# The first FFN's down projection computed as 2x2 blocks with seven block products

## The chip, the cores and the metric

The kernel runs on one core of a Trainium2 chip. The metric is the device time of one execution in microseconds (us), as a median of repeated executions; beside it stands one execution that the hardware profiler recorded. Engines are named as the profile names them: PE (TensorE, matmuls), PEld (its weight loads), DVE (VectorE), ACT (ScalarE), POOL (GpSimd), SP (SyncE, which here only issues DMAs).

## The reference

One residual block on 512 tokens of width 1024: a feed-forward part (FFN1), a token mixer, and a second feed-forward part (FFN2), each between RMS norms. The change touches the first of these lines:

```python
def swiglu(x, w_gu, w_down):
    g, u = jnp.split(x @ w_gu, 2, axis=-1)
    return (jax.nn.silu(g) * u) @ w_down

f = swiglu(rms_norm(h, ffn1_pre_g[l]), ffn1_w_gu[l], ffn1_w_down[l])
h = h + MACARON_SCALE * rms_norm(f, ffn1_post_g[l])
m = hybrid_mixer(rms_norm(h, mix_pre_g[l]), ...)
```

The hidden width (ff) is 2816, which is 22 chunks of 128. `w_down` is 2816 by 1024.

## The kernel before

**Numbers.** Every fp32 operand is split into a high part (rounded to the fp32r type, an ACT copy) and a low part (what is left, a DVE subtract). One product is three matmuls: high by high, high by low, low by high (`mm3`, lines 134 to 137). Each new operand therefore costs one cast on ACT and one subtract on DVE before PE can use all of it. Weights come in the order of a list (`worder`), through a small set of buffers: SP loads `wraw`, ACT and DVE make `w` (`wsplit`, lines 101 to 109).

**FFN1, gate and up.** The first 6 pairs of ff chunks ("standard", tiles f1f and f1g) are ordinary products; the other 16 pairs go in `paired` (tiles f1X, f1Y, f1Q) as 2x2 blocks with seven products instead of eight. The tiles f1W are its split weights, f1M and f1N sums of weight blocks, and u1m and u1ts the sums and splits of the normalised input that this form needs. The hidden activations end in tiles f1p, four chunks in each.

**FFN1, down.** `token_out` (lines 585 to 617) walks over the 22 ff chunks. For each chunk it takes one weight w (128 by 1024) and the split chunk of activations (ph, pl), and for four token blocks and two halves of the output it runs `mm3` with 512 columns into eight accumulators f1o. The last 6 chunks (`TAILS[0]`) are held back: they are run token block by token block, so that the first block is complete early and its norm (`boundary`, name b1) runs beside the matmuls of the others. The b1 work of a token block is `post_norm` (a square with a sum on ACT, a scale on DVE for each half, then a small chain over DVE and POOL), `normalise`, and transposes on PE back to feature order (`to_features`, tiles b1ntp into u2h and u2l), from which the mixer's first products x start.

**FFN2, down.** It is already done in the other form, by the class `Blocked` (lines 469 to 579). Sixteen ff chunks form two groups; in each group the product of the (tokens by ff) block and the (ff by outputs) block is cut in 2x2 blocks, and seven block products replace eight. A product is four steps (two groups, two halves), 28 steps in all. Each step needs a split weight block f2w, and each product a split sum of activations f2a (`prep`); then `multiply` runs 12 matmuls with 512 columns into banks X, Y, Z and V. Between products, `add_up` adds weight blocks and activation blocks on DVE, POOL adds a weight block from memory with an accumulating DMA (line 538), and `snap` copies a bank aside when a product has to count in two outputs. At the end `post_norm` adds or subtracts that copy first (tile b3qz, line 213). The 6 ordinary chunks left over go into the same banks, the first two for all tokens, the last four token by token (`TAILS[2]` is 4). The steps of `Blocked` are issued in the order of the program text (`manual_schedule`); elsewhere a scheduler sets the order of each engine's queue.

**Short loads for the mixer.** `vec`, `sink`, `cs` and `msk` are loaded by SP after the fifth ordinary down weight (line 751); `hb` (DVE, line 758) and `z` (ACT, line 763) are the first users of `vec`.

Of the kernel before, what the change touches and what calls it, by code (L numbers as in the profile page):

```python
# [16 lines left out]
P = 128  # L17
LRU_LAG = (2, 2)
ATT_LAG = (3, 2)
TAILS = (6, 7, 4)  # L20
JSTD = {"f1": 6, "f2": 4}
GC = 4
NS = 4 * GC
LEAD = 3
PRODUCTS = (1, 2, 5, 6, 3, 7, 4)
BLOCKED = ("f2",)
FEATURE_LAG = {"b1": (3, 3, 3, 3), "b2": (3, 3, 3, 4)}
ATT_GATES = (2, 3, 4, 5, 6, 7)
T = 512
# [11 lines left out]


@with_exitstack
def hybrid_block_kernel(ctx, tc, x, xt, g1, w_first, gains, gu1, gs1, dn1, w_x, w_gate, w_q, w_k, w_v, w_gl, w_ga, w_pl, w_pa,
                        w_o, gu2, gs2, dn2, ds2, vecs, bd, sinks, rope, mask, out):
    nc = tc.nc
    V, A, G, PE, SP = nc.vector, nc.scalar, nc.gpsimd, nc.tensor, nc.sync
# [204 lines left out]
    def gate_up(u, name, first, fast, rs=None, ds=None):  # L252
        ps = {}
        sp = []
        base = NS if ds is not None else 0

        def pw(j):
            if j < base:
                key, slot, n = (j // (2 * GC), j % 2), j // 2 % GC, GC
            else:  # L260
                key, slot, n = (j - base) // 4, (j - base) % 4, 4
            if key not in ps:
                ps[key] = b8(f"{name}p{j}", [P, n, T])
            return ps[key][:, slot, :]

        def split(c):
            i = c - base
            if i % 4 == 0:
                sp.append((b8(f"{name}ph{i // 4}", [P, 4, T], F32R), b8(f"{name}pl{i // 4}", [P, 4, T], F32R)))
            split_chunk(ps[i // 4], *sp[-1], i % 4)  # L270

        def chunk(c):
            if c + 2 < KF and c >= base + 2:
                split(c + 2)
            return sp[(c - base) // 4]

        def tail(j, bg, bu):
            s = t2(f"{name}s{j}")
            if rs is not None:
                gs, us = t2(f"{name}gs{j}"), t2(f"{name}us{j}")  # L280
                V.tensor_tensor(out=gs, in0=bg, in1=rs(), op=ALU.mult)
                V.tensor_tensor(out=us, in0=bu, in1=rs(), op=ALU.mult)
                bg, bu = gs, us
            A.activation(s, bg, AF.Tanh, scale=0.5)
            V.scalar_tensor_tensor(out=s, in0=s, scalar=1.0, in1=bg, op0=ALU.add, op1=ALU.mult)
            V.scalar_tensor_tensor(out=pw(j), in0=s, scalar=0.5, in1=bu, op0=ALU.mult, op1=ALU.mult)

        bs = []

        def done(i, b):  # L290
            bs.append(b)
            if i % 2 == 1:
                tail(i // 2, bs[i - 1], b)

        first(u, f"{name}f", done)
        for j in range(2, JSTD[name]):
            bb = []
            for i in range(2):
                w = wget()
                b = bank(f"{name}g{j}{i}")  # L300
                feat_chunk(b, w, u, ALL)
                tick()
                bb.append(b)
            tail(j, *bb)
        while live:
            tick()
        blocked = None if ds is None else Blocked(name, ps, ds)
        ahead = iter(range(base, base + 4))
        paired(fast(), name, pw, blocked, lambda: split(next(ahead)))
        if blocked is None:  # L310
            for c in range(4):
                split(c)
        return chunk, blocked
# [305 lines left out]
    def boundary(src, dst, g_post, g_pre, u, scale, name, raw=None, then=None):  # L619
        rhs = []  # L620

        def residual():
            t = len(rhs)
            if t < NT:
                rh = b8(f"{name}rh{t}", [P, 2, D])
                A.dma_start(rh[:, 0, :], src[t])
                rhs.append(rh)

        residual()
        residual()  # L630

        def epilogue(t, banks, fix):
            residual()
            h = post_norm(banks, fix, t, g_post, rhs[t], scale, f"{name}q", dst[t] if g_pre is None else None)
            if g_pre is None:
                return
            un = normalise(h, t4(f"{name}un{t}"), t, g_pre, f"{name}n")
            A.dma_start(dst[t], h)
            yield FEATURE_LAG[name][t]
            to_features(un, t, u, f"{name}n", raw)  # L640
            if then is not None and t == NT - 1:
                start(then())

        return epilogue
# [93 lines left out]
        wsplit(2)  # L738
        start(token_scale(lambda: [done(i, b) for i, b in enumerate(bs)]))

    chunk1, _ = gate_up(u1, "f1", first_unscaled, lambda: (gs1, mv1), lambda: rbc)
    g_post, g_pre = gain_pair(1, 2, "g_b1")
    u2 = new_u("u2")
    hs = [dram.tile([P, D], F32, name=f"h_spill{t}") for t in range(NT)]
    token_out(chunk1, KF, boundary(xv, hs, g_post, g_pre, u2, 0.5, "b1"), "f1", TAILS[0])

    vec = const.tile([P, 8, KD], F32, name="vec")
    sink = const.tile([P, NH], F32, name="sink")
# [322 lines left out]
def _layout(inputs):  # L1071
    import numpy as np

    c = np.ascontiguousarray
    f = {k: np.asarray(v)[0] for k, v in inputs.items()}
    a = {}
    a["x"] = c(f["x"])
    a["xt"] = c(f["x"].T.reshape(KD, P, T))
    a["g1"] = c(f["ffn1_pre_g"].reshape(KD, P).T)
    a["w_first"] = None  # L1080
    a["gains"] = np.stack([f[n] for n in ("ffn1_pre_g", "ffn1_post_g", "mix_pre_g", "mix_post_g",
                                          "ffn2_pre_g", "ffn2_post_g")])

    def gu(w):
        return c(w.reshape(KD, P, 2, KF, P).transpose(3, 2, 1, 0, 4).reshape(KF, 2, P, D))

    def chunks(w):
        return c(w.reshape(KD, P, KD, P).transpose(2, 1, 0, 3).reshape(KD, P, D))

    a["w_first"] = c(f["ffn1_w_gu"].reshape(KD, P, 2, KF, P)[:, :, :, :2].transpose(0, 1, 3, 2, 4).reshape(KD, P, 512))  # L1090
    def pairs_of(w, j):
        b = w.reshape(2, 4, P, 2, KF // 2, 2, P).transpose(4, 3, 5, 0, 2, 1, 6)[j // 2:].reshape(-1, 2, 2, P, 512)
        return c(np.stack([np.concatenate([b[:, 0, 1], b[:, 0, 0]], 2), np.concatenate([b[:, 1, 0], b[:, 1, 1]], 2)], 1))

    a["gu1"], a["gs1"] = gu(f["ffn1_w_gu"])[2:JSTD["f1"]], pairs_of(f["ffn1_w_gu"], JSTD["f1"])
    a["dn1"] = c(f["ffn1_w_down"].reshape(KF, P, D))
    w = f["w_in"]
    a["w_x"], a["w_gate"] = chunks(w[:, D:2 * D]), chunks(w[:, :D])
    half = HD // 2

    def pairs(w):
        return w.reshape(D, -1, 4, 2, half).transpose(0, 1, 3, 2, 4).reshape(D, -1)

    def chunks_of(w):
        n = w.shape[1] // P
        return c(w.reshape(KD, P, n, P).transpose(2, 1, 0, 3).reshape(n, P, D))

    a["w_q"], a["w_k"] = chunks_of(pairs(w[:, 2048:3072])), chunks_of(pairs(w[:, 3072:3328]))
    a["w_v"] = c(w[:, 3328:3584].reshape(2, 4, P, 256).transpose(0, 2, 1, 3).reshape(2, P, 1024))
    a["w_gl"], a["w_ga"] = chunks(w[:, 3584:4608]), chunks(w[:, 4608:])  # L1110
    a["w_pl"] = chunks(f["w_proj_lru"])
    wa = f["w_proj_attn"].reshape(2, 2, 4, HD, D).transpose(0, 2, 1, 3, 4).reshape(D, D)
    a["w_pa"] = chunks(wa)
    a["w_o"] = c(f["w_out"].reshape(KD, P, D))
    a["gu2"], a["gs2"] = gu(f["ffn2_w_gu"])[:JSTD["f2"]], pairs_of(f["ffn2_w_gu"], JSTD["f2"])
    a["dn2"] = c(f["ffn2_w_down"].reshape(KF, P, D)[NS:])

    def quarters(w):
        b = w[:NS * P].reshape(2, 2, 2, 2, P, 2, 512)
        return c(b.transpose(0, 5, 3, 1, 4, 2, 6).reshape(2, 2, 2, 2, P, 1024))  # L1120

    q = quarters(f["ffn2_w_down"])
    a["ds2"] = c(np.stack([q[:, 0, 0], q[:, 1, 0], q[:, 0, 1], q[:, 1, 1]], 1))
    vec = [f["conv_w"][i] for i in range(4)] + [f[n] for n in _VECS]
    a["vecs"] = c(np.stack(vec).reshape(8, KD, P).transpose(2, 0, 1))
    bd = np.zeros((2, 2, HD, KD, 2, HD), np.float32)
    wb = np.stack([f["lru_w_a"], f["lru_w_x"]]).reshape(2, KD, 2, HD, HD)
    for r in range(2):
        bd[:, r, :, :, r, :] = wb[:, :, r].transpose(0, 2, 1, 3)
    a["bd"] = bd.reshape(2, P, D)  # L1130
    a["sinks"] = f["attn_sinks"]
    inv = (10000.0 ** (-np.arange(half) / half)).astype(np.float32)
    ang = np.arange(T, dtype=np.float32)[:, None] * inv[None, :]
    cs = np.stack([np.cos(ang), np.sin(ang)]).astype(np.float32).transpose(2, 0, 1)
    a["rope"] = c(np.tile(cs, (4, 1, 1)))
    qi, si = np.arange(P)[:, None], np.arange(2 * P)[None, :]
    a["mask"] = np.where((si > qi) & (si <= qi + P), 0.0, -1e30).astype(np.float32)
    return a
# [24 lines left out]
```

## Time and profile before

| | |
|---|---|
| median of 3 runs | 1149.4 us (1148.77 to 1150.24) |
| the profiled execution | 1149.67 us, of which its span is 1147.9 us |
| mean granted PE clock | 0.995 |
| ACT busy | 558.2 us (49% of the span) |
| POOL busy | 64.4 us (6%) |
| FFN1 start (first products, scaling) | to about 86 us |
| FFN1 gate and up, paired | 86 to 243.2 us |
| FFN1 down | 243.2 to 369.5 us |
| FFN2 gate and up, paired | 850 to 1026.4 us |
| FFN2 down, blocked | 1026.4 to 1097.5 us, then its tail to 1140 us |

The profile is of one execution. A row of a timeline has the start, the duration, the engine, the line, the operation, and output<-inputs with their shapes; in brackets stands the idle time before it and what ended that. [...] A row of the windows has, for each engine, the busy time in that stretch and the number of instructions, then the granted clock, the share of the DMA engines and GB/s.

### The profile page before, as it was taken

What the parts mean: (1) busy time and instruction counts of PE and PEld (TensorE: products, weight loads), DVE (VectorE), ACT (ScalarE), POOL (GpSimd) and SP (SyncE); (2) the same over time, 40 slices, a digit from 0 to 9 for tenths busy, and PEclk for the clock granted to TensorE, in tenths of its full rate; (3) what the DMA queues carried; (4) which work ended last, traced back from release to release, by engine and by line L of the source; (5) the groups of instructions that cost most, each with busy time, mean ns of one, the idle gap of its engine ahead of it and who ended that gap; (6) DMA issues with size and microseconds to landing.
All of it is one profiled execution on the core that took longest, in us unless ns stands there. A gap on an engine that the chain in (4) does not pass through costs nothing.

```text
span 1147.9 us, 16623 instructions
## 1 busy us (share of the span) xinstructions
PE 1121.6 (98%) x6632; PEld 999.0 (87%) x6632; DVE 847.0 (74%) x1216; ACT 558.2 (49%) x942; POOL 64.4 (6%) x66
## 2 busy tenths in 40 slices
PE   7979999999999999999999999999999999999997
PEld 6769999998888988888888888887989999998886
DVE  6598889975315787999867662455758989979866
ACT  7234545553313676566655441344435555455652
POOL 1000000000001010212211100000000000001000
PEclk9999999999999999999999999999999999999999
DMA  9123333274312545432632432432313333255632
GB/s 362 46 69 111 111 107 98 84 285 167 93 37 99 180 142 148 151 90 73 194 118 74 147 114 88 165 128 100 122 37 111 111 108 97 90 184 159 171 128 74
DMA packets 41757, 142.81 MB, mean 124 GB/s; under 512 B 5072, under 2 KB 5200, under 8 KB 41040
## 3 DMA queue, kind: packets, MB, share of 16 engines
q1 hardware_dynamic: 35920, 122.35, 33.2%
q10 hardware_dynamic: 4608, 15.21, 3.6%
q0 software_dynamic: 1152, 4.19, 1.9%
q8 instruction: 52, 0.85, 0.3%
q14 instruction: 25, 0.20, 0.1%
HBM read 130.20 MB, written 11.53 MB: 123 GB/s over the span
## 4 chain that ended last, share of the span: by engine, by line
PE 85%; DVE 10%; ACT 2%; issue 2%; DMA 1%; POOL 0%; DVEq 0%; POOLq 0%; ACTq 0%
PE f2X L136 4%; PE f2X L137 4%; PE f2X L135 4%; PE f1o L135 3%; PE f1o L137 3%; PE f1o L136 3%; PE f1X L135 3%; PE f1X L137 3%; PE f1X L136 3%; PE f1f L736 2%; PE f2Q L137 2%; PE f2Q L136 2%; PE f2Q L135 2%; DVE w L106 1%; PE f1Q L135 1%
## 5 line engine op out<-in xcount | busy, mean ns | idle before, releaser
L106 DVE TENSOR_TENSOR w<-wraw,w 128x1024 fp32r<-128x1024 f32 x112 | 136.4, 1248 | 44.8 <-ACT w L105 43.4
L105 ACT CAST w<-wraw 128x1024 fp32r<-128x1024 f32 x112 | 112.9, 1049 | 64.8 <-PE f1o L137 17.7
L135 PE MATMUL f1X<-u1m,f1W 128*128 128x256 f32 x256 | 73.1, 286 | 3.7 <-ACT f1sn L365 3.7
L137 PE MATMUL f1X<-u1m,f1W 128*128 128x256 f32 x256 | 73.2, 286 | 2.3 <-DVE f1W L345 2.3
L136 PE MATMUL f1X<-u1m,f1W 128*128 128x256 f32 x256 | 73.0, 285 | 0.0
L135 PE MATMUL f1o<-w,f1ph 128*128 128x512 f32 x176 | 68.5, 390 | 0.0
L136 PE MATMUL f1o<-w,f1ph 128*128 128x512 f32 x176 | 68.5, 389 | 0.0
L137 PE MATMUL f1o<-w,f1pl 128*128 128x512 f32 x176 | 67.0, 389 | 0.0
L135 PEld LDWEIGHTS f1X<-u1m,f1W 128*128 128x128 f32 x256 | 49.7, 194 | 4.0 <-ACT f1sn L365 3.9
L137 PEld LDWEIGHTS f1X<-u1m,f1W 128*128 128x128 f32 x256 | 49.6, 194 | 2.6 <-DVE f1W L345 2.5
L136 PEld LDWEIGHTS f1X<-u1m,f1W 128*128 128x128 f32 x256 | 49.7, 194 | 0.1
L137 PE MATMUL f2X<-u3m,f2W 128*128 128x256 f32 x144 | 40.8, 283 | 0.0
L137 PE MATMUL f2Q<-u3m,f2W 128*128 128x256 f32 x144 | 40.8, 283 | 0.0
L135 PE MATMUL f2Q<-u3m,f2W 128*128 128x256 f32 x144 | 40.8, 283 | 0.0
L136 PE MATMUL f2X<-u3l,f2W 128*128 128x256 f32 x144 | 40.8, 283 | 0.0
L137 PE MATMUL f2X<-u3h,f2W 128*128 128x256 f32 x144 | 40.8, 283 | 0.0
L136 PE MATMUL f2X<-u3m,f2W 128*128 128x256 f32 x144 | 40.8, 283 | 0.0
L136 PE MATMUL f2Q<-u3m,f2W 128*128 128x256 f32 x144 | 40.8, 283 | 0.0
L135 PE MATMUL f2X<-u3m,f2W 128*128 128x256 f32 x144 | 40.7, 283 | 0.0
L135 PE MATMUL f2X<-u3h,f2W 128*128 128x256 f32 x144 | 40.7, 283 | 0.0
L135 PEld LDWEIGHTS f1o<-w,f1ph 128*128 128x128 f32 x176 | 33.0, 188 | 6.9 <-ACT f1ph L249 0.2
L136 PEld LDWEIGHTS f1o<-w,f1ph 128*128 128x128 f32 x176 | 33.0, 188 | 6.9
(784 smaller groups left out, 3703.7 us busy)
## 6 DMA issues: line engine op xcount, KB each, us to landing
wraw<-in_dn_dram SPq DMA_DIRECT2D x28, 512.0 KB, 5.3
f2L<-in_gs_dram SPq DMA_DIRECT2D x18, 512.0 KB, 3.6
f2R<-in_gs_dram SPq DMA_DIRECT2D x18, 512.0 KB, 4.4
wraw<-in_gu_dram SPq DMA_DIRECT2D x16, 512.0 KB, 6.4
f1L<-in_gs_dram SPq DMA_DIRECT2D x16, 512.0 KB, 3.6
f1R<-in_gs_dram SPq DMA_DIRECT2D x16, 512.0 KB, 4.3
f2b<-in_ds_dram SPq DMA_DIRECT2D x16, 512.0 KB, 4.5
wraw<-in_w_x_dram SPq DMA_DIRECT2D x8, 512.0 KB, 4.5
```

The source lines that it names most:

```text
L105: A.copy(w[:, 0, :], raws[n])
L106: V.tensor_tensor(out=w[:, 1, :], in0=raws[n], in1=w[:, 0, :].bitcast(F32), op=ALU.subtract)
L135: PE.matmul(o, lhsT=ah, rhs=bh, start=start, stop=False, skip_group_check=reopen)
L136: PE.matmul(o, lhsT=ah, rhs=bl, start=False, stop=False, skip_group_check=reopen)
L137: PE.matmul(o, lhsT=al, rhs=bh, start=False, stop=stop, skip_group_check=reopen)
L736: PE.matmul(bs[i], lhsT=lw[:, i * P:(i + 1) * P], rhs=rx, start=k == 0 and n == 0, stop=k == KD - 1 and n == 2)
```

## The change

The class `Blocked` is given to FFN1 as well. `gate_up` gets the rearranged weights `ds1`; the host rearranges both down weights with one helper, `down`, and `dn1` now holds only 6 chunks.

```diff
-    chunk1, _ = gate_up(u1, "f1", first_unscaled, lambda: (gs1, mv1), lambda: rbc)
+    chunk1, blocked1 = gate_up(u1, "f1", first_unscaled, lambda: (gs1, mv1), lambda: rbc, ds1)
...
-    token_out(chunk1, KF, boundary(xv, hs, g_post, g_pre, u2, 0.5, "b1"), "f1", TAILS[0])
+    token_out(chunk1, KF, boundary(xv, hs, g_post, g_pre, u2, 0.5, "b1"), "f1", TAILS[0], blocked1)
...
-    a["dn1"] = c(f["ffn1_w_down"].reshape(KF, P, D))
+    a["dn1"], a["ds1"] = down(f["ffn1_w_down"])
...
-    a["dn2"] = c(f["ffn2_w_down"].reshape(KF, P, D)[NS:])
+    a["dn2"], a["ds2"] = down(f["ffn2_w_down"])
```

Since `TAILS[0]` stays 6 and six ordinary chunks are left, all six now run token by token. The 528 ordinary matmuls f1o become 480: 336 in the 28 steps (tiles f1X, f1Y, f1Z, f1V) and 144 in the tail. On DVE come 28 splits f1w, 14 splits f1a, 8 sums of activations, 8 sums of weights and 8 corrections b1qz; 16 splits of w and 16 of f1pl go. On ACT come 28 casts f1w, 14 casts f1a and 8 copies of a bank, and 16 casts of w and 16 of f1ph go. POOL gets 8 accumulating DMAs of 512 KB; SP gets 16 loads f1b and loses 16 loads wraw. One line lower than before stands everything below line 26 of the kernel, since an unused constant is gone.

Giving `ds1` also changes how `pw` places the activations: the tile f1p that a chunk is written to is now chosen by even and odd chunk, as `Blocked` reads them, and that shifts the scheduler's order in the first stage, whose code is the same. These are rows of DVE's queue in that first stage, before (w4 and w5 are the split weights of the standard chunk 4; f1gs, f1us, f1s, f1p steps of a chunk's activation; u1ts, u1m parts of the input for the paired products):

```order
L286 SCALAR_TENSOR_TENSOR f1p0_395<-f1s0_388,f1us0_390 128x512
L106 TENSOR_TENSOR w4_417<-wraw4_272,w4_417 128x1024
L659 TENSOR_TENSOR u1ts1_525<-xs1_78,u1ts0_524 128x1024
L281 TENSOR_TENSOR f1gs3_486<-f1g30_422,rbc_124 128x512
L106 TENSOR_TENSOR w5_451<-wraw5_321,w5_451 128x1024
L286 SCALAR_TENSOR_TENSOR f1p0_395<-f1s1_397,f1us1_399 128x512
```

And the same place of DVE's queue after the change:

```order
L285 SCALAR_TENSOR_TENSOR f1p0_395<-f1s0_388,f1us0_390 128x512
L658 TENSOR_TENSOR u1ts1_526<-xs1_78,u1ts0_525 128x1024
L280 TENSOR_TENSOR f1gs3_487<-f1g30_423,rbc_124 128x512
L284 SCALAR_TENSOR_TENSOR f1s2_410<-f1s2_410,f1gs2_411 128x512
L285 SCALAR_TENSOR_TENSOR f1p1_404<-f1s1_397,f1us1_399 128x512
L281 TENSOR_TENSOR f1us3_488<-f1g31_455,rbc_124 128x512
L105 TENSOR_TENSOR w4_418<-wraw4_272,w4_418 128x1024
L105 TENSOR_TENSOR w5_452<-wraw5_321,w5_452 128x1024
```

The split of w4 has moved behind one operation of 1024 columns and four of 512. Some thirty rows further on, at the entry of the paired stage, DVE's queue before reads (f1W20 is the weight of the third product of pair 0):

```order
L286 SCALAR_TENSOR_TENSOR f1p4_573<-f1s5_629,f1us5_631 128x512
L334 TENSOR_TENSOR f1M0_649<-f1R0_638,f1L0_637 128x512
L334 TENSOR_TENSOR f1M1_663<-f1R1_642,f1L1_641 128x512
L334 TENSOR_TENSOR f1N0_650<-f1R0_638,f1M0_649 128x512
L334 TENSOR_TENSOR f1N1_664<-f1R1_642,f1M1_663 128x512
L345 TENSOR_TENSOR f1W20_658<-f1M0_649,f1W20_658 128x1024
L345 TENSOR_TENSOR f1W11_669<-f1R1_642,f1W11_669 128x1024
```

After the change the same place reads:

```order
L333 TENSOR_TENSOR f1M0_649<-f1R0_638,f1L0_637 128x512
L281 TENSOR_TENSOR f1us5_631<-f1g51_604,rbc_124 128x512
L333 TENSOR_TENSOR f1M1_663<-f1R1_642,f1L1_641 128x512
L333 TENSOR_TENSOR f1N0_650<-f1R0_638,f1M0_649 128x512
L284 SCALAR_TENSOR_TENSOR f1s5_629<-f1s5_629,f1gs5_630 128x512
L344 TENSOR_TENSOR f1W20_658<-f1M0_649,f1W20_658 128x1024
L333 TENSOR_TENSOR f1N1_664<-f1R1_642,f1M1_663 128x512
L344 TENSOR_TENSOR f1W11_669<-f1R1_642,f1W11_669 128x1024
L370 TENSOR_TENSOR f1ca0_701<-f1Y0_673,f1sn0_699 128x256
L285 SCALAR_TENSOR_TENSOR f1p1_404<-f1s5_629,f1us5_631 128x512
```

Two operations of 512 columns, the sum f1N1 and the last f1p of chunk 5, now stand behind the split of f1W20, which so comes earlier by these two. The third place is the end of the blocked steps on DVE, where the six ordinary weights w8 to w13 are split (f1w411 is the last blocked weight; hb reads vec):

```order
L534 TENSOR_TENSOR f1w411_3140<-f1b111_2482,f1w411_3140 128x1024
L249 TENSOR_TENSOR f1pl0_3117<-f1p16_2235,f1ph0_3116 128x512
L757 TENSOR_SCALAR hb_3531<-vec_3523 128x16
L105 TENSOR_TENSOR w8_3157<-wraw8_3062,w8_3157 128x1024
L249 TENSOR_TENSOR f1pl0_3117<-f1p16_2235,f1ph0_3116 128x512 x2
L105 TENSOR_TENSOR w9_3194<-wraw9_3064,w9_3194 128x1024
L105 TENSOR_TENSOR w10_3215<-wraw10_3066,w10_3215 128x1024
L105 TENSOR_TENSOR w11_3220<-wraw11_3160,w11_3220 128x1024
L105 TENSOR_TENSOR w12_3225<-wraw12_3197,w12_3225 128x1024
L249 TENSOR_TENSOR f1pl1_3231<-f1p20_2710,f1ph1_3230 128x512 x2
L105 TENSOR_TENSOR w13_3234<-wraw13_3218,w13_3234 128x1024
```

Before, the split of an ordinary weight stood well ahead of its use all along the stage, and hb stood between two of them near its start:

```order
L373 TENSOR_TENSOR f1cb15_2522<-f1Q15_2482,f1sw15_2620 128x256
L758 TENSOR_SCALAR hb_3489<-vec_3481 128x16
L106 TENSOR_TENSOR w10_2677<-wraw10_2586,w10_2677 128x1024
L106 TENSOR_TENSOR w11_2714<-wraw11_2591,w11_2714 128x1024
L106 TENSOR_TENSOR w12_2743<-wraw12_2596,w12_2743 128x1024
```

Now hb, and with it the wait for vec's load, stands directly ahead of w8, and the other five splits follow it in one run.

More of the change, by code (lines that the diff above doesn't have):

```diff
@@ L25 @@
 PRODUCTS = (1, 2, 5, 6, 3, 7, 4)
-BLOCKED = ("f2",)
 FEATURE_LAG = {"b1": (3, 3, 3, 3), "b2": (3, 3, 3, 4)}
@@ L43, in hybrid_block_kernel @@
 @with_exitstack
-def hybrid_block_kernel(ctx, tc, x, xt, g1, w_first, gains, gu1, gs1, dn1, w_x, w_gate, w_q, w_k, w_v, w_gl, w_ga, w_pl, w_pa,
+def hybrid_block_kernel(ctx, tc, x, xt, g1, w_first, gains, gu1, gs1, dn1, ds1, w_x, w_gate, w_q, w_k, w_v, w_gl, w_ga, w_pl, w_pa,
                         w_o, gu2, gs2, dn2, ds2, vecs, bd, sinks, rope, mask, out):
@@ L1095, in _layout, with down @@
     a["gu1"], a["gs1"] = gu(f["ffn1_w_gu"])[2:JSTD["f1"]], pairs_of(f["ffn1_w_gu"], JSTD["f1"])
-    a["dn1"] = c(f["ffn1_w_down"].reshape(KF, P, D))
+    def down(w):
+        b = w[:NS * P].reshape(2, GC // 2, 2, 2, P, 2, 512).transpose(0, 5, 3, 1, 4, 2, 6).reshape(2, 2, 2, 2, P, 1024)
+        return c(w.reshape(KF, P, D)[NS:]), c(np.stack([b[:, 0, 0], b[:, 1, 0], b[:, 0, 1], b[:, 1, 1]], 1))
+    a["dn1"], a["ds1"] = down(f["ffn1_w_down"])
     w = f["w_in"]
@@ L1115, in _layout @@
     a["gu2"], a["gs2"] = gu(f["ffn2_w_gu"])[:JSTD["f2"]], pairs_of(f["ffn2_w_gu"], JSTD["f2"])
-    a["dn2"] = c(f["ffn2_w_down"].reshape(KF, P, D)[NS:])
[L1118 to L1123, printed above, removed]
+    a["dn2"], a["ds2"] = down(f["ffn2_w_down"])
     vec = [f["conv_w"][i] for i in range(4)] + [f[n] for n in _VECS]
```

## The prediction

> **What bounds the kernel now.** I read the page first: the busy shares, then the chain that ended last.
>
> ```profile
> PE 1121.6 (98%) x6632; PEld 999.0 (87%) x6632; DVE 847.0 (74%) x1216; ACT 558.2 (49%) x942; POOL 64.4 (6%) x66
> PE 85%; DVE 10%; ACT 2%; issue 2%; DMA 1%; POOL 0%; DVEq 0%; POOLq 0%; ACTq 0%
> ```
>
> PE is the bound over the whole, but 10% of the chain is DVE, so the average hides a stage with another limit. The windows, stage by stage, show which (start of FFN1, its down projection, FFN2's blocked down projection, and the token tail behind that):
>
> ```profile
> 43.00:86.00 43.00, 35.16 (x164) 28.91 (x163) 43.00 (x57) 17.34 (x22) 0.00 (x0) 1.00 0.17 49
> 243.20:369.50 126.30, 125.92 (x580) 104.97 (x580) 61.68 (x94) 45.41 (x74) 3.83 (x7) 1.00 0.37 131
> 1026.40:1097.50 71.10, 70.71 (x329) 58.71 (x328) 63.72 (x63) 42.70 (x50) 7.11 (x8) 1.00 0.55 146
> 1097.50:1140.00 42.50, 42.50 (x189) 35.18 (x189) 26.38 (x37) 12.98 (x25) 1.66 (x3) 1.00 0.30 111
> ```
>
> In the stage that is changed PE idles 0.38 of 126.3 us and DVE is half used (61.68): fewer matmuls shorten it one for one. FFN2, which already has the new form, is PE-bound too, but DVE works 63.72 of 71.1 us there. Between 43 and 86 us DVE is busy without a gap and PE waits. Last, the list of PE's waits:
>
> ```profile
> PE f1X L135 <- ACT f1sn L365: 3.7, 1, 3.7
> PE f1X L137 <- DVE f1W L345: 2.3, 1, 2.3
> PE f1g L137 <- DVE w L106: 1.9, 1, 1.9
> PE x L135 <- ACT u2h L199: 0.6, 2, 0.4
> PE f2X L136 <- DVE f2w L535: 0.4, 1, 0.4
> ```
>
> The first three lie in the start of FFN1; the blocked form has cost FFN2's PE one wait of 0.4 us.
>
> **The matmuls that go.** 528 become 480: 48 of 128x512 less. Their price is a distance between starts, not a duration. The page's group has the duration; the window is a stretch of the down projection in which PE does little else:
>
> ```profile
> L135 PE MATMUL f1o<-w,f1ph 128*128 128x512 f32 x176 | 68.5, 390 | 0.0
> 260.00:340.00 80.00, 80.00 (x355) 66.26 (x354) 29.80 (x39) 24.61 (x32) 0.00 (x0) 1.00 0.30 98
> ```
>
> 80 us over 355 matmuls is 0.2254 us each, against a duration of 0.390. So 48 x 0.2254 = 10.8 us. [...]
>
> **The 28 steps.** They add to DVE and ACT, and that work has to hide under 336 matmuls, 336 x 0.2254 = 75.7 us. FFN2 runs the same list of steps, with the same waits in its queues, so its rows price them: the split of a step, its share of the accumulating DMAs.
>
> ```profile
> L535 DVE TENSOR_TENSOR f2w<-f2b,f2w x28: 1212/1219/1226, 1019.4 to 1099.0; 128x1024 fp32r<-128x1024 f32 x28
> ACT f2w L534 <- DMA f2b<-in_ds_dram: 6.7, 3, 2.6
> ```
>
> DVE gets 28 + 14 + 8 + 8 operations of 1.22 us, 70.8 us, and beside them its share of the last paired products; it is nearly full, as in FFN2. ACT waited 6.7 us there for accumulated weights, and of all this 0.4 us reached PE, since steps are prepared three ahead. I take 0.4 us again; bounds 0 and, with one such DMA wait (2.6 us) reaching PE, 3 us.
>
> **The token tail.** Six weights must be there for the first token block, where FFN2 had two spread over all tokens and four. FFN2's end of the steps shows what DVE does behind the last blocked split and when PE is through with the steps:
>
> ```profile
> 1097.90 2.35 DVE L535 TENSOR_TENSOR f2w<-f2b,f2w 128x1024 fp32r<-128x1024 f32 x2
> 1100.77 1.21 DVE L106 TENSOR_TENSOR w<-wraw,w 128x1024 fp32r<-128x1024 f32 x1
> 1103.11 4.62 DVE L106 TENSOR_TENSOR w<-wraw,w 128x1024 fp32r<-128x1024 f32 x4
> 1107.65 1.28 DVE L250 TENSOR_TENSOR f2pl<-f2p,f2ph 128x512 fp32r<-128x512 f32 x2
> 1108.86 1.21 DVE L106 TENSOR_TENSOR w<-wraw,w 128x1024 fp32r<-128x1024 f32 x1
> ...
> 1108.67 0.39 PE L137 MATMUL f2V<-f2w,f2a 128*128 128x512 f32 x1
> ```
>
> Two splits in 2.35 us are one every 1.13, two of 512 columns in 1.28 one every 0.60; those steps are used below. The last blocked split ends at 1100.25 and the last step on PE near 1108.9, so PE is 8.7 us behind DVE. After it DVE needs 9.8 us for six splits and four small ones (1108.86 + 1.21 - 1100.25), in nearly the order that FFN1 now gets. PE takes the sixth weight only after five others in both halves or more: 18 matmuls for a half of a token block are 4.1 us, and the order puts the sixth weight 6.4 us into the tail. So it is wanted 8.7 + 6.4 = 15.1 us after the last blocked split and is there after about 9.9: slack about 5 us. New is the head-of-line wait: hb waits for vec's load directly ahead of w8, and behind hb all six splits are queued, and behind those PE. The load is issued after the fifth ordinary weight, about 5 us before hb, and took this long before:
>
> ```profile
> L752 SPq DMA_DIRECT2D vec<-in_vecs_dram x1: 424/424/424, 231.1 to 231.1; - x1
> DMA to landing us min/median/max: 6.2/6.2/6.2
> ```
>
> So DVE may stand up to 1.2 us at hb, inside the slack. SP's queue itself only issues. ACT's z waits for the same load ahead of w13's cast, with the same slack. I count 0; if the load comes more than 5 us late, the rest is lost one for one.
>
> **The norm behind it.** Each half now starts with a correction b1qz on DVE. FFN2 shows its price, and FFN1's last token block before shows the chain into the mixer:
>
> ```profile
> L213 DVE TENSOR_TENSOR b3qz<-f2X,f2s x2: 691/692/692, 1135.4 to 1140.8; 128x512 f32<-128x512 f32 x2
> 367.74 0.69 DVE L215 SCALAR_TENSOR_TENSOR b1rh<-f1o,g_b 128x512 f32<-128x512 f32 x1 [2.14 <-ACT b1qsq L214]
> 368.35 0.20 DVE L218 TENSOR_SCALAR b1qpe<-b1qps 128x1 f32<-128x1 f32 x1
> 369.66 1.28 DVE L221 SCALAR_TENSOR_TENSOR b1rh<-b1rh,b1qpr 128x1024 f32<-128x1024 f32 x1
> 373.10 1.28 DVE L187 SCALAR_TENSOR_TENSOR b1un<-b1rh,b1nr,g_b 128x1024 f32<-128x1024 f32 x1 [0.73 <-POOL b1nr L172]
> ...
> 374.97 1.04 PE L195 MATMUL b1ntp<-ident,b1un 128*128 128x128 f32 x8
> ```
>
> Before, the square came first and the scale waited for it; now both follow the correction at once, so the chain grows by little of the 0.69. But DVE's queue now holds one more split of another token block (0.6 us a step) ahead of the pe step and one more ahead of the rh step: about 1.1 us later in all. PE came to the last block's transposes at 374.97 (row below the four), 0.6 us after b1un was done (373.10 + 1.28 = 374.38), so 0.5 us of it reaches PE. With what PE's short waits for u2h can lengthen I take +0.6; bounds -0.3 (they shorten) and +2 (both splits and the whole correction show).
>
> **The start, reordered.** DVE sets the pace there, so what is put behind what decides. The rows that the order of the queue moves:
>
> ```profile
> 54.48 1.22 DVE L106 TENSOR_TENSOR w<-wraw,w 128x1024 fp32r<-128x1024 f32 x1
> ...
> 85.34 1.22 DVE L345 TENSOR_TENSOR f1W<-f1M,f1W 128x1024 fp32r<-128x1024 f32 x1
> ...
> 76.74 0.28 PE L135 MATMUL f1X<-u1m,f1W 128*128 128x256 f32 x1
> 76.86 0.28 PE L136 MATMUL f1X<-u1m,f1W 128*128 128x256 f32 x1
> 86.04 0.58 PE L135 MATMUL f1X<-u1m,f1W 128*128 128x256 f32 x1 [3.68 <-ACT f1sn L365]
> 86.64 0.56 PE L137 MATMUL f1X<-u1m,f1W 128*128 128x256 f32 x1
> 88.91 0.35 PE L135 MATMUL f1Q<-u1m,f1W 128*128 128x256 f32 x1
> ...
> 83.73 1.04 ACT L344 CAST f1W<-f1M 128x1024 fp32r<-128x1024 f32 x1 [7.82 <-DVE f1M L334]
> ...
> 85.65:89.00 3.35, 2.96 (x13) 2.89 (x14) 3.35 (x4) 1.28 (x3) 0.00 (x0) 0.50 0.39 101
> 82.20:85.60 3.40, 0.16 (x2) 0.00 (x0) 3.40 (x7) 1.87 (x2) 0.00 (x0) 1.00 0.01 2
> ```
>
> Loss first: w4's split, at 54.48 before, now stands behind one operation of 1024 columns (1.13) and four of 512 (0.60), 3.5 us later. PE then waits about 5 us for it instead of 1.9, and the granted clock may halve for one stretch behind that, as it did from 85.65 to 89.0 after PE had been nearly idle from 82.2 to 85.6: about 1.3 us more. With w4 split at 54.48 + 3.5 + 1.2 = 59.2, 90 ordinary matmuls (90 x 0.2254 = 20.3) and 1.3 for the half clock, the ordinary part ends on PE at 80.8 us, 4.1 later than before (76.74). But from there PE waits anyway. Gain second: two operations of 0.6 us move behind the split of f1W20, which so starts at 84.1, not 85.34, and its cast on ACT comes earlier too. The third matmul of product 6 (86.64) waits for that split, so it comes at about 85.4; it now runs at the full clock, ten left at 0.12 us (76.74 to 76.86), and the next product starts at 86.6 instead of 88.91: -2.3 us. Bounds: -3 (the first wait is also shorter than I think) and +1 (the late PE pushes the entry by more than DVE gains).
>
> [...]
>
> **Sum.** -10.8 + 0.4 + 0 + 0.6 - 2.3 = -12.1 us. From the profiled execution, 1149.67 us, that makes 1137.6; the median of the runs shown, 1149.4, is 0.3 us below that execution, which I leave inside the range. About 0.2%, 2.3 us, is what a measurement of this kernel can tell from no change.
>
> **The rivals.**
>
> 1. The start gives nothing back or costs. For it: PE is 4.1 us late and the margin to DVE there is small, since f1us5 needs the late product f1g51. Against it: DVE has no gap in the stage, and its sequence to f1W20 is shorter. Then -9.8 or, at the bound, -8.8: 1139.9 to 1140.9.
> 2. The tail starves: vec, or the six loads of the weights, land late, and every split behind hb with them. For it: the wait is new and six splits hang on it. Against: 5 us of slack. With 4 to 9 us over the slack, the sum is -8 to -3: 1141.6 to 1146.6.
> 3. Slower than before: the accumulating DMAs set the pace of FFN1's steps. There are 8, each between a DVE split and the next use of that weight. If each held PE for the longest of FFN2's ACT waits, 2.6 us, that is 21 us, and the time 1137.6 + 21 = 1158.6. It decides from 1.5 us each. For it: DMA share 0.55 in FFN2's stage. Against: there 0.4 us in all reached PE.
> 4. A matmul costs its duration. Then 48 x 0.390 = 18.7 us go, and the time is 1129.7. Against it: the starts.
> [...]
>
> That the 48 matmuls do not go is no rival: the queue of PE has them no more.
>
> **How the numbers follow.** Forecast 0.56; rival 1 0.22; rival 2 0.10; rival 3 0.04; rival 4 0.05; rival 5 0.03. The likeliest is 1137.6. Its own range is from 1134.8 (start -3, norm -0.3, steps 0, and the median's 0.3 and 0.7 of run-to-run) to 1140. To hold 8 in 10 it must take rival 1 whole and the near part of rival 2: 1134.5 to 1143. Faster by over 0.2%: all but rival 3 and the far end of rival 2, 0.94; same 0.02; slower 0.04.
>
> **What would show it.** In the profile after: the stretch from the first paired matmul of the down stage to the mixer's first x shorter by 10 to 11 us; the granted clock at half near 58 us and full at 86; the first f1Q product 2 to 3 us earlier; no PE wait above 1 us between the steps; the row of hb with at most about 1 us of idle time and no wait of PE for w behind it; the waits for u2h longer by about 0.5 us. Wrong it would be with a PE wait for f1w or for w of several us, with f1Q no earlier than before, or if a matmul saved is worth other than 0.22 to 0.23 us.

## The result

| | before | after |
|---|---|---|
| median | 1149.82 us (1148.77 to 1150.35, 4 runs) | 1137.32 us (1136.59 to 1137.87, 4 runs) |
| profiled execution | 1149.67 us, span 1147.9 | 1137.61 us, span 1135.8 |

The ratio is 0.9892, with a 95% interval of 0.9875 to 0.9909: 12.5 us faster, where 12.1 were forecast (1137.6). Of the executions reported below one, of e8_p7_spread, took 3922 us and is left out of its figures. First the page after, its busy shares:

```profile
span 1135.8 us, 16614 instructions
...
PE 1111.3 (98%) x6584; PEld 987.5 (87%) x6584; DVE 889.9 (78%) x1250; ACT 579.2 (51%) x960; POOL 72.0 (6%) x74
```

PE has 48 matmuls less (6584 for 6632) and is still the bound; DVE has 43 us more. The windows after, for the start of FFN1, the 28 steps of its down projection, its token tail, and most of FFN2's steps (they run to 1096.9 us; before, to 1108.9, past the end of the window that the prediction gave them):

```profile
43.00:86.00 43.00, 38.34 (x170) 30.47 (x169) 43.00 (x56) 18.37 (x22) 0.00 (x0) 0.96 0.16 49
239.52:322.30 82.78, 82.03 (x378) 67.91 (x377) 74.93 (x76) 52.38 (x64) 7.17 (x8) 1.00 0.61 173
322.30:355.00 32.70, 32.70 (x150) 27.09 (x150) 24.88 (x48) 10.40 (x24) 3.69 (x6) 1.00 0.38 151
1013.79:1084.00 70.21, 69.42 (x322) 57.18 (x321) 62.13 (x61) 41.20 (x48) 6.98 (x8) 1.00 0.55 143
```

FFN1's steps look like FFN2's: DVE fills 74.93 of 82.78 us and PE idles 0.75. In the tail PE has no gap. PE's waits after, those that answer to the ones shown before:

```profile
PE f1g L134 <- ACT w L104: 3.8, 3, 2.1
PE f2X L135 <- DVE f2w L534: 0.8, 2, 0.4
PE f1X L135 <- DVE f1w L534: 0.8, 2, 0.4
PE f1X L136 <- DVE f1W L344: 0.7, 1, 0.7
PE x L134 <- ACT u2h L198: 0.5, 2, 0.2
PE f1X L134 <- ACT f1sn L364: 0.2, 1, 0.2
```

The wait for w has doubled (1.9 to 3.8), the two at the entry to the paired stage have shrunk from 6.0 to 0.9, and new are two of 0.4 for f1w. Where the time came from is read by laying the same matmul of both traces side by side. The rows after that mark the places (the first f1Q product, the first transposes behind the tail, the first of FFN2's paired products and of its steps):

```profile
86.88 0.28 PE L134 MATMUL f1Q<-u1m,f1W 128*128 128x256 f32 x1
354.99 1.03 PE L194 MATMUL b1ntp<-ident,b1un 128*128 128x128 f32 x8
836.68 0.28 PE L134 MATMUL f2X<-u3h,f2W 128*128 128x256 f32 x1
1013.79 0.40 PE L134 MATMUL f2X<-f2w,f2a 128*128 128x512 f32 x1
```

And those of them before that the prediction didn't show:

```profile
366.82 1.04 PE L195 MATMUL b1ntp<-ident,b1un 128*128 128x128 f32 x8
849.41 0.28 PE L135 MATMUL f2X<-u3h,f2W 128*128 128x256 f32 x1
1026.52 0.40 PE L135 MATMUL f2X<-f2w,f2a 128*128 128x512 f32 x1
```

| part | shift at its end | of this part | forecast |
|---|---|---|---|
| start of FFN1 to f1Q | -2.0 (-2.1 a pair later) | -2.1 | -2.3 |
| paired stage | -2.1 | 0 | 0 |
| steps and tail to the first transposes | 366.82 to 354.99: -11.8 | -9.7 | -10.8 + 0.4 |
| norm, to the last token block's transposes | 374.97 to 363.26: -11.7 | +0.1 | +0.6 |
| mixer, to FFN2's first matmul | 800.64 to 789.36: -11.3 | +0.4 | 0 |
| FFN2's first products | 849.41 to 836.68: -12.7 | -1.4 | 0 |
| FFN2's steps to the end of the span | 1147.9 to 1135.8: -12.1 | +0.6 | 0 |

The forecast terms were each right to within 0.7 us. That the sum of the traces, -12.1, is the forecast to a tenth is luck: the errors of the terms (+0.2, +0.7 and -0.5) and three parts that were not forecast (+0.4, -1.4, +0.6) nearly cancel.

### The profile page after: what moved, and what is told of

The parts are those of the page before. It is cut to its first block, busy times and chain, and to the rows that moved or that the text cites. A ratio compares the mean times of both kernels' runs of the same rounds, so it can differ in the third digit from the quotient of the medians.

```text
span 1135.8 us, 16614 instructions
## 1 busy us (share of the span) xinstructions
PE 1111.3 (98%) x6584; PEld 987.5 (87%) x6584; DVE 889.9 (78%) x1250; ACT 579.2 (51%) x960; POOL 72.0 (6%) x74
## 4 chain that ended last, share of the span: by engine, by line
PE 54%; DVE 9%; issue 2%; DMA 1%; ACT 1%; POOL 0%; DVEq 0%; POOLq 0%; ACTq 0%
PE f2X L135 4%; PE f2X L136 3%; PE f2X L134 3%; PE f2Q L136 1%; PE f2Q L135 1%; PE f2Q L134 1%; PE glg L134 1%; PE glp L134 1%; PE glp L136 1%; PE glg L136 1%; PE glg L135 1%; PE glp L135 1%; PE gap L135 1%; PE gag L135 1%; PE gag L136 1%
## 5 line engine op out<-in xcount | busy, mean ns | idle before, releaser
L105 DVE TENSOR_TENSOR w<-wraw,w 128x1024 fp32r<-128x1024 f32 x96 | 117.0, 1253 | 17.3 <-ACT w L104 15.9
L104 ACT CAST w<-wraw 128x1024 fp32r<-128x1024 f32 x96 | 96.6, 1049 | 24.5 <-PE glp L136 7.3
L534 DVE TENSOR_TENSOR f2w<-f2b,f2w 128x1024 fp32r<-128x1024 f32 x28 | 33.9, 1219 | 5.0 <-ACT f2w L533 5.0
L534 DVE TENSOR_TENSOR f1w<-f1b,f1w 128x1024 fp32r<-128x1024 f32 x28 | 33.9, 1220 | 4.8 <-ACT f1w L533 4.8
L134 PE MATMUL f1Q<-u1m,f1W 128*128 128x256 f32 x128 | 36.2, 283 | 0.0
L135 PE MATMUL f1Q<-u1m,f1W 128*128 128x256 f32 x128 | 36.2, 283 | 0.0
L136 PE MATMUL f1Q<-u1m,f1W 128*128 128x256 f32 x128 | 36.2, 283 | 0.0
```

The lines of the kernel that those rows point to most:

```text
L104: A.copy(w[:, 0, :], raws[n])
L105: V.tensor_tensor(out=w[:, 1, :], in0=raws[n], in1=w[:, 0, :].bitcast(F32), op=ALU.subtract)
L134: PE.matmul(o, lhsT=ah, rhs=bh, start=start, stop=False, skip_group_check=reopen)
L135: PE.matmul(o, lhsT=ah, rhs=bl, start=False, stop=False, skip_group_check=reopen)
L136: PE.matmul(o, lhsT=al, rhs=bh, start=False, stop=stop, skip_group_check=reopen)
L534: V.tensor_tensor(out=w[:, 1], in0=z, in1=w[:, 0].bitcast(F32), op=ALU.subtract)
```

## The experiments

The theory after the result: 48 matmuls at the distance of starts, a start that gains by DVE's order, and steps that lose a little at product 7, where a step needs three DVE operations. Rivals: the start was chance, the matmuls have another price, the accumulating DMAs are what the steps wait for.

**The placement alone (e1_layout_only), on the kernel before.**

```diff
-            if j < base:
-                key, slot, n = (j // (2 * GC), j % 2), j // 2 % GC, GC
-            else:
-                key, slot, n = (j - base) // 4, (j - base) % 4, 4
+            key, slot, n = place(j)   # f1: as the changed kernel places chunks 0 to 15
```

> The kernel before, with only the placement of FFN1's activations as in the changed kernel (tiles f1p by even and odd chunk); all 528 down matmuls stay. DVE's queue in the first stage is then that of the changed kernel. Theory A (the start gains by the order of DVE's queue): the first f1Q product at about 86.9 us instead of 88.9, and 2.1 us less in all, about 1147.5 against 1149.6. Rival B (the earlier start was chance, a granted clock that happened to fall elsewhere): f1Q at 88.9, and no change. Either way FFN2's start may differ by up to 1.5 us with the phase of the granted clock.

Measured: 1146.25 us (before 1149.65), ratio 0.9971 with an interval of 0.9961 to 0.9982. Two rows of its trace, at the entry to the paired stage:

```profile
85.74 0.38 PE L137 MATMUL f1X<-u1m,f1W 128*128 128x256 f32 x1 [0.66 <-DVE f1W L351]
87.04 0.28 PE L135 MATMUL f1Q<-u1m,f1W 128*128 128x256 f32 x1
```

f1Q comes at 87.04: rival B falls, the placement alone, with the order of the queues that it brings, is worth 1.9 us in the trace. The two profiled executions differ by 3.5 us in all, and 1.4 of the rest lie in FFN2's start (below); the medians differ by 3.4.

**The blocked form without the placement (e4_rows_layout).** The blocks are cut by neighbouring chunks, so the tiles and DVE's first queue are those of before.

```diff
                 key, slot, n = (j // (2 * GC), j % 2), j // 2 % GC, GC
+                if name == "f1":
+                    key, slot = (j // (2 * GC), j // GC % 2), j % GC
...
+            b = w[:NS * P].reshape(2, 2, GC // 2, 2, P, 2, 512).transpose(0, 5, 1, 2, 4, 3, 6).reshape(2, 2, 2, 2, P, 1024)
```

> The changed kernel with the 2x2 blocks of FFN1 cut so that a tile f1p holds four neighbouring chunks, as before the change; the weights are rearranged to match, and all 480 matmuls stay. DVE's queue in the first stage is then that of the kernel before. Theory A: f1Q at 88.9 us again, the time 2.1 us above the changed kernel, about 1139.4, a gain of 10 us over before. Rival B: 1137.3, as the changed kernel.

Measured: 1139.8 us, ratio 0.9918 (0.9906 to 0.9931). The same place of its trace:

```profile
86.07 0.58 PE L134 MATMUL f1X<-u1m,f1W 128*128 128x256 f32 x1 [3.70 <-ACT f1sn L366]
...
88.94 0.40 PE L134 MATMUL f1Q<-u1m,f1W 128*128 128x256 f32 x1
```

The wait of 3.7 us and f1Q at 88.94 are back, as in the kernel before. With e1 this is a square of four kernels: the placement is worth 3.4 us without the blocked form and 2.5 with it, the blocked form 9.9 without the placement and 8.9 with it. The two parts add, within the spread of a run.

**48 matmuls left out (e2_48_fewer), of the kernel before.**

```diff
-        PE.matmul(o, lhsT=ah, rhs=bl, start=False, stop=False, skip_group_check=reopen)
+        if not two:   # two: f1, chunks 4 to 9
+            PE.matmul(o, lhsT=ah, rhs=bl, start=False, stop=False, skip_group_check=reopen)
```

> The kernel before, leaving out 48 matmuls of 128x512: the second one (high by low) of chunks 4 to 9 in the down projection of FFN1; its output lacks these parts. Loads, splits and all else stay. [...]

Measured: 1138.61 us, 11.0 less, ratio 0.9906 (0.9893 to 0.992). That is 0.23 us for each, the distance between starts that the forecast counted with (48 x 0.2254 = 10.8): the next matmul begins before the last has ended. The mean duration (48 x 0.390 = 18.7) is out. In its trace the shift from the paired stage to the first x is 10.9 us, 48 x 0.227; the whole shows it so well because two parts that are not of the 48, +1.2 us in the paired stage and -1.4 at FFN2's start, cancel. The same trace shows why the old start order costs more in some executions than in others:

```profile
84.40:91.10 6.70, 5.68 (x26) 5.61 (x27) 5.35 (x7) 4.48 (x7) 0.00 (x0) 0.50 0.48 158
```

Here the half clock behind the idle time at the entry lasted two stretches (6.8 us from 84.35) and not one, and the paired stage lost 1.2 us more against the kernel before (its shift goes from -0.6 at f1Q to +0.6 at its end). With the new order the half clock falls at 58 us in this place's stead, where PE waits for DVE afterwards anyway: in after_again, a second profile of the changed kernel, it lasted two stretches there (from 55.84 to 62.67), and f1Q came at 87.08, only 0.2 us later.

**Product 7's sums by DMA (e5_p7_dma).**

```diff
-            if i == 7:
-                z = self.raw[5, g, h]
-                V.tensor_tensor(out=z, in0=z, in1=self.raw[3, g, h], op=ALU.add)
+                G.dma_start(self.raw[5, g, h], self.ds[g, 3, h], accum_op=ALU.add)   # after product 5's sum
```

> The changed kernel, where the weight sum of product 7 is no longer made by DVE (8 additions of 128x1024, 4 in each FFN) but by 8 more accumulating DMAs of POOL, issued as soon as product 5's sum has been read. Theory A (the steps of product 7 stall since DVE needs three operations of 1.13 us for a step of 2.7 us on PE): the two stalls of FFN1 (1.1 us) and the ones of FFN2 (0.7 to 1.2 us) go, 1.5 to 2 us less, about 1135.6. Rival C (the accumulating DMAs set the pace of the steps): no gain, or new waits of PE for f1w, 1137 to 1140.

Measured: 1152.05 us, 14.7 above the changed kernel and slower than before, ratio 1.0026 (1.0015 to 1.0037). The same stretch of FFN1's steps in its windows, a wait of ACT, one of PE, and POOL's landing time:

```profile
262.00:297.00 35.00, 30.40 (x120) 23.53 (x119) 22.93 (x21) 13.95 (x15) 8.73 (x10) 0.90 1.06 247
...
ACT f1w L531 <- DMA f1b<-in_ds_dram: 15.2, 4, 6.5
...
282.54 0.80 PE L134 MATMUL f1X<-f1w,f1a 128*128 128x512 f32 x1 [3.07 <-ACT f1w L531]
...
f1b<-in_ds_dram POOLq DMA_DIRECT2D x12, 512.0 KB, 12.0
```

For comparison the changed kernel in the same stretch:

```profile
262.00:297.00 35.00, 35.00 (x156) 28.96 (x156) 30.95 (x28) 20.00 (x22) 7.17 (x8) 1.00 0.89 220
...
ACT f1w L533 <- DMA f1b<-in_ds_dram: 7.2, 3, 2.7
...
f1b<-in_ds_dram POOLq DMA_DIRECT2D x8, 512.0 KB, 9.0
```

Four more accumulating DMAs in a stage that uses 0.89 of the DMA engines bring them to 1.06, landing goes from 9.0 to 12.0 us, ACT waits twice as long, PE stops for 3 us and then runs at half clock (0.50 from 282.40 to 289.20). The stop is at the second step of product 6. Its accumulating DMA was issued as early as in the changed kernel (265.83 and 265.80), but ACT's cast of the weight came at 281.45 and not at 274.67. So rival C's mechanism is real, close by, and theory A's remedy was the wrong one. It is also rival 3 of the prediction, with its price: 7.0 us in FFN1 for four more.

**The same sums earlier on DVE (e8_p7_spread, e8_again).**

```diff
+            if i == 6 and h == 1:
+                V.tensor_tensor(out=hi(0), in0=hi(0), in1=lo(0), op=ALU.subtract)
+            if (i, h) in ((3, 1), (7, 1)):
+                z = self.raw[5, g, 0 if i == 3 else 1]
+                V.tensor_tensor(out=z, in0=z, in1=self.raw[3, g, 0 if i == 3 else 1], op=ALU.add)
```

> The changed kernel, where the same DVE additions for product 7 are done earlier, in both FFNs: the activation sum of product 7 during product 6, and half of its weight sums during product 3. Nothing is added, no DMA moves. Theory A (product 7 stalls PE since DVE has three operations of 1.13 us per step there): the stalls of 1.1 us in FFN1 and 0.7 to 1.2 us in FFN2 go, about 1135.5. Rival C (the stalls are lateness inherited from the accumulating DMAs, earlier in the steps): no change, 1137.3, since the same work reaches the same place late.

> The earlier additions for product 7 again, now with more runs: the first trace had 0.9 us less in FFN1's steps and 0.2 us less in FFN2's. If that is so, 1.0 us below the changed kernel, about 1136.3; if it was chance, the same.

Measured: 1136.02, 1136.08 and 1138.37 us, ratio 0.9882 (0.9866 to 0.9899) the first time; the second time 1136.18 us (1135.99 to 1136.68), ratio 0.9882 (0.9867 to 0.9897), beside the changed kernel on the same chip, after_again:

> The changed kernel once more, beside the next three on the same chip. By the parts found so far: 12 us faster than before, some 1137.3 us, and single runs spread by about 1.5 us with the stretches at half clock.

That gave 1137.47 us (1136.96 to 1138.43), 0.9893 (0.9879 to 0.9908). By the medians it is 1.3 us, and in this pair no run of the one lies in the range of the other (the first time one did, 1138.37). The traces show less: the two profiled executions are 0.7 us apart, 0.6 of it in FFN1's steps, and next to nothing is gained in FFN2's. The list of PE's waits has none for f1w left, but the starts show that the stalls of product 7 have moved, smaller in FFN1, to product 3 there and in FFN2 to products 6 and 3:

```profile
287.53 0.39 PE L134 MATMUL f1Z<-f1w,f1a 128*128 128x512 f32 x1
288.04 0.50 PE L135 MATMUL f1Z<-f1w,f1a 128*128 128x512 f32 x1
288.38 0.39 PE L136 MATMUL f1Z<-f1w,f1a 128*128 128x512 f32 x1
...
1062.23 0.50 PE L135 MATMUL f2Z<-f2w,f2a 128*128 128x512 f32 x1 [0.40 <-DVE f2w L536]
```

Counted between starts, PE loses 0.5 to 0.6 us to them in FFN1, where the changed kernel loses 1.2 to 1.3, and 1.2 to 1.3 us in FFN2, where it loses 1.2 to 1.5. So theory A's forecast fails in FFN2, and half of it in FFN1. ACT's wait for the accumulated weights is nearly as long as before:

```profile
ACT f1w L535 <- DMA f1b<-in_ds_dram: 6.8, 3, 2.6
```

**Without the accumulating DMAs (e9_no_accum).**

```diff
-            if i in (5, 6):
+            if i in (5, 6) and self.name == "f2":
                 G.dma_start(first, self.ds[g, 3 if i == 5 else 2, h], accum_op=ALU.add)
```

> The changed kernel without the eight accumulating DMAs of FFN1's steps; the weights of four of its products lack a term, all other instructions stay. Theory A: the two stalls of PE at product 7 (0.53 and 0.55 us) stay. Rival C: they go, and ACT's waits for f1b (7.2 us) with them; 1.1 us less.

Measured: a single execution, 1137.43 us, with FFN2's first products at half clock in it (its mean granted clock is 0.994; the changed kernel's profiled execution has 0.998). In FFN1's steps its trace has no wait of PE for f1w, though product 7 has its three operations per step; the stage is 1.4 us shorter than in the changed kernel. The stretch from the steps to the first x has this one wait of PE left:

```profile
PE x L134 <- ACT u2h L198: 0.2, 1, 0.2
```

So the accumulating DMAs are needed for FFN1's stalls: without them none is left, with product 7's load in place, as rival C said. DVE's load decides where and how large they show, by e8: less work at product 7 makes them smaller in FFN1 and moves them. How it comes about is argued and not shown step by step: the waits for the accumulated weights eat the lead of three steps, and where DVE's work is dense it is not made up. Rows of the changed kernel show the two stalls:

```profile
301.06 0.39 PE L134 MATMUL f1X<-f1w,f1a 128*128 128x512 f32 x1
301.81 0.50 PE L135 MATMUL f1X<-f1w,f1a 128*128 128x512 f32 x1 [0.37 <-DVE f1w L534]
302.15 0.39 PE L136 MATMUL f1X<-f1w,f1a 128*128 128x512 f32 x1
...
305.22 0.50 PE L135 MATMUL f1X<-f1w,f1a 128*128 128x512 f32 x1 [0.39 <-DVE f1w L534]
```

Two steps from 301.06 to 302.15 take 1.09 us where two undisturbed ones take 0.45: a wait listed with 0.37 costs 0.64 between starts, since the matmul behind it also starts late. The second costs 0.66 in the same way; together 1.3 us, and e9's stage gained 1.4.

**Four chunks in the tail (e3_tail4).** The edit is `TAILS = (4, 7, 4)`.

> The changed kernel with four instead of six chunks in FFN1's token tail, two going to all tokens first, as in FFN2. If the six weights of the tail are in time (as forecast), no gain: 1137.3, or later, since the norm of a token block then has 5.4 us of matmuls beside it and not 8.1. If the tail starved, 1 us or more faster.

Measured: 1139.7 us, ratio 0.9907 (0.989 to 0.9923), 2.4 above the changed kernel. The tail ends at the same time (its last matmul is 0.03 us apart), so nothing starved; the norm shows instead:

```profile
356.91 0.38 PE L134 MATMUL x<-u2h,w 128*128 128x256 f32 x1 [0.86 <-ACT u2h L198]
357.84 0.39 PE L135 MATMUL x<-u2l,w 128*128 128x256 f32 x1 [0.55 <-DVE u2l L199]
365.15 1.09 PE L194 MATMUL b1ntp<-ident,b1un 128*128 128x128 f32 x8 [0.56 <-DVE b1un L186]
```

With six chunks these three were 0.2, none and 0.1. Leaving the tail at six when only six chunks remained was right.

**Two tries to shorten the start further (e7_sums_pool, e12_late_sums, e11_both).** e7 gives the eight sums of the first two pairs to POOL:

```diff
-                V.tensor_tensor(out=o, in0=a, in1=b, op=ALU.add)
+                (G if name == "f1" and k < 2 else V).tensor_tensor(out=o, in0=a, in1=b, op=ALU.add)
```

> The changed kernel, where the eight weight sums of the first two pairs in FFN1 (f1M, f1L, f1N of 512 columns) are made by POOL instead of DVE. If DVE's queue sets the pace of the start, 8 x 0.60 = 4.8 us leave it, of which PE can use only the two short waits left at its entry to the paired stage (0.8 us), since the late split of w4 stays where it is: about 1136.5, f1Q 0.8 us earlier. If POOL is slow at it (several us each) or holds DVE up, later than 1137.3.

Measured: 1140.55 us, ratio 0.9914 (0.99 to 0.9929), slower by 3.2. POOL needs 1.3 to 3.9 us for what takes DVE 0.69, and f1Q comes at 89.30:

```profile
76.02 3.94 POOL L333 TENSOR_TENSOR f1M<-f1R,f1L 128x512 f32<-128x512 f32 x1 [50.19 <-DVE u1m L654]
80.04 1.28 POOL L333 TENSOR_TENSOR f1L<-f1L 128x512 f32<-128x512 f32 x1
85.02 2.27 POOL L333 TENSOR_TENSOR f1N<-f1R,f1M 128x512 f32<-128x512 f32 x1
...
89.30 0.41 PE L134 MATMUL f1Q<-u1m,f1W 128*128 128x256 f32 x1
```

e12 puts pair 1's sums behind the split of f1W20; e11 is e12 with e8's edit.

```diff
+            late = name == "f1" and k == 0
-            if d < n:
+            if d < n and not late:
                 sums(d)
                 parts(d, 1)
...
+                if late:
+                    sums(d)
+                    parts(d, 1)
                 product(6, k, False)
```

> The changed kernel, where in FFN1 the weight sums and the first split of pair 1 (four operations of 512 columns and one of 1024 on DVE, one cast on ACT) come after the third product's weight f1W20 of pair 0 and not before it. If DVE's order sets the entry to the paired stage, the two waits there (0.2 us for f1sn, 0.7 us for f1W20) go and nothing else changes, as PE is then bound by its own late end of the standard part: f1Q at 86.1 us instead of 86.9, 0.8 us less. If pair 1 then comes late, PE waits one pair later and the gain is lost.

> Both edits: the earlier additions for product 7 and the later sums of pair 1. If they add, 1.8 us below the changed kernel, about 1135.5, below both kernels of this study.

Measured: 1140.25 us (0.9916, 0.9901 to 0.9931) and 1139.12 us (0.9904, 0.9887 to 0.992); by their medians both slower than the changed kernel, though e11's runs (1137.22 to 1140.7) overlap with its. f1Q did come 1.2 us earlier in e12, but pair 1 was late:

```profile
85.67 0.28 PE L134 MATMUL f1Q<-u1m,f1W 128*128 128x256 f32 x1
...
89.37 0.43 PE L136 MATMUL f1X<-u1m,f1W 128*128 128x256 f32 x1 [1.86 <-DVE f1W L344]
```

The wait moved on to the next pair, grew to 1.9 us, and a stretch at half clock began at 89.56, on the paired stage that PE bounds: behind the wait the starts lie 0.21 us apart (89.60, 89.81), ahead of it 0.12 (87.11, 87.23). By its median e8 is the best version that was run.

## Why the prediction was right, point by point

- **The matmuls, -10.8.** Right, shown twice: 11.0 us of the stage's shift (-9.7, less the 1.3 of the stalls), and 10.9 in e2's trace. The step was the right price; rival 4 is out, and so is a price well below the step: each one left out saved 0.23 us in e2's median and 0.227 in its trace.
- **The 28 steps, +0.4.** Right that little of the new work reaches PE; the size is too small: 1.3 us, two stalls at product 7. The term that was mis-sized took FFN2's listed wait of 0.4 us over as the whole cost, but such a wait costs 0.65 between starts. FFN2 shows one such wait before the change and two after it, so one trace did not give their number either. The bounds (0 to 3) held.
- **The token tail, 0.** Right. hb had no wait: vec landed 3.5 us after its issue at 309.0, and DVE came to hb at 314.24. PE had no gap in the tail.
- **The norm, +0.6.** Too much by half a microsecond. b1un of the last block came 0.65 us later after the end of the tail and not 1.1, and the reserve of 0.6 us in front of the transposes hid nearly all of it: +0.1. Of the two splits that were to stand ahead, only one did (0.60, ahead of the pe step), and the correction cost nothing: the scale of the first half starts 1.16 us after the tail's last matmul in both traces (367.74 after 366.58; 355.91 after 354.75), since before it waited for the square. PE's waits for u2h did not grow (0.6 before, 0.5 after).

```profile
355.91 0.69 DVE L214 SCALAR_TENSOR_TENSOR b1rh<-b1qz,g_b 128x512 f32<-128x512 f32 x1
```

- **The start, -2.3.** Right in its gain and nearly in each time: the half clock from 58.6 to 62.0, f1X at 81.2 (forecast 80.8), the split of f1W20 at 84.31 (84.1), the third matmul at 85.59 (85.4), f1Q at 86.88 (86.6). The loss ahead of it took another path than the forecast one. PE was to wait about 5 us for w4's split on DVE; it waited 3.8 in three parts, each for a cast of a weight on ACT. The first two of these casts began at 53.58 and not at 50.41, since in ACT's queue they now stand behind one more step f1s of an activation, which waits for DVE. e1 and e4 show that the start hangs on the placement, and so on the order of the queues. Rival 1 is out.

```profile
53.04 0.63 ACT L283 ACTIVATE f1s<-f1gs 128x512 f32<-128x512 f32 x1 [2.36 <-DVE f1gs L280]
...
58.70:62.00 3.30, 3.30 (x8) 2.16 (x8) 3.30 (x4) 3.30 (x4) 0.00 (x0) 0.50 0.37 129
...
84.31 1.22 DVE L344 TENSOR_TENSOR f1W<-f1M,f1W 128x1024 fp32r<-128x1024 f32 x1
...
85.59 0.39 PE L136 MATMUL f1X<-u1m,f1W 128*128 128x256 f32 x1 [0.66 <-DVE f1W L344]
```

- **What was not forecast.** The mixer's +0.4 stands in this trace at a new wait of q for DVE; it is in most traces of the blocked form and not in e9 and e5, and its cause stays open. The +0.6 of FFN2's steps is the second stall there. FFN2's -1.4 is the granted clock: before, PE's gap ahead of FFN2's first products brought 3.4 us at half clock; after, the same gap did not. These are the two stretches, before and after:

```profile
802.45:805.80 3.35, 3.26 (x15) 3.27 (x16) 3.02 (x5) 2.66 (x5) 0.12 (x1) 0.50 0.91 349
```

```profile
791.20:794.60 3.40, 3.34 (x28) 3.34 (x29) 2.99 (x5) 2.72 (x5) 0.10 (x1) 1.00 0.96 347
```

Of the 14 traces of this study four show it, with the new form and without, so the blocked form alone doesn't decide it. How much of the 12.5 us in the medians is of this kind isn't settled. It isn't only the traced pair: the 28 executions of the kernel before that were run beside the experiments have a mean granted clock of 0.994 to 0.996, the eight of the changed kernel 0.995 to 0.998. By the parts that the change owns it is -2.1 - 9.7 + 0.1 = -11.7 in the traces, and the medians' start is worth more than the traces' by up to one more stretch at half clock (e2, e1).

- **Rival 3**, the accumulating DMAs, was rightly held small but is nearer than "0.4 us in all" made it look: four more per FFN made the kernel slower than before.

## What to carry to other kernels

Price a removed matmul by the distance between starts in the stage it leaves, and a stage that gets a known form by the waits that form shows elsewhere, counted between starts and not by the idle time alone. A change that touches no line of a stage can still move its order through the names or keys of tiles that it shares: compare the queues, and let the engine that is busy without a gap decide. A stall can show where one engine is crowded and be owed to a delay several steps earlier: when the work there was spread it moved, and when the delay was gone it went. Count what all stalls of a stage cost together, not the one at the old place, and add no load to what is already full.

## What the runs showed of the hardware that I had not expected

- Accumulating DMAs: at a DMA share of 0.89, four more of 512 KB per FFN raised the landing time from 9.0 to 12.0 us and cost 7.0 us in FFN1 (the shift of the first x goes from -12.0 to -5.0).
- After PE's idle time the half clock lasted one stretch of 3.4 us in most traces and two (6.8 us) in others of the same order of work: two from 84.35 in e2 and from 55.84 in after_again, one only from 85.63 before and from 58.63 after. At FFN2's start, gaps of 1.5 and 0.4 us brought it in four of 14 traces. In each trace the half stretches begin whole multiples of 3.413 us apart (before, 85.63 and 802.43: 210 of them). On that grid the four traces are those in which one step holds both gaps, 1.8 to 1.9 us idle; in the other ten no step there holds more than 1.55. These are such steps, the first followed by half clock (before), the second not (e3):

```profile
799.02:802.43 3.41, 1.61 (x13) 1.29 (x11) 3.41 (x6) 2.98 (x7) 0.40 (x1) 1.00 0.74 239
...
789.36:792.77 3.41, 1.87 (x15) 1.42 (x13) 3.41 (x6) 2.99 (x7) 0.14 (x1) 1.00 0.61 219
```

  All 23 half stretches that begin in the 14 traces between 12 us and the last 7 us follow a step with PE idle for 1.72 us or more, about half of it (before, 3.27 ahead of 85.63 and 1.80 ahead of 802.43; after, 2.32 ahead of 58.63; with the ends of matmuls as the profile models them); of the steps at full clock with as much idle time only one, in e4's start (1.80), was not followed by half clock.

- POOL took 1.3 to 3.9 us for an addition of 128x512 (e7) that takes DVE 0.69 (after).
